# Weight buffers 4,608 bytes apart, and the operands of token-major blocks at one place of a 512-byte line

## The chip, the core and the metric

The kernel runs on one core of one Trainium2 chip. The metric is the time of one execution on the device, in microseconds (us): the median of several runs.

## What is computed

One decoder layer in float32, 256 tokens of 2048 features, with three residual steps: a mixer (chunked mLSTM beside an RWKV-7 scan, each gated and merged), cross-attention into 256 memory tokens, and a convolutional GeGLU network. Nearly all of the arithmetic is projections by large weight matrices:

```python
proj = h @ w_in                                   # 2048 x 10536
merged = sigmoid(g_a) * (ha @ w_branch_a) + sigmoid(g_b) * (hb @ w_branch_b)
y = merged @ w_out                                # 2048 x 2048
q, kv = h @ wq, mem_n @ wkv                       # cross-attention, then o @ wo
u = h @ w_up                                      # 2048 x 16384
uc = conv_b + sum(conv_w[j] * shift_right(u, 2 - j) for j in range(3))
gate, up = split_cols(uc, (8192, 8192))
out = (gelu(gate) * up) @ w_down                  # 8192 x 2048
```

## The kernel before

**Blocks.** The projections are a list of blocks, filled by `block(...)` and worked off in order by `run()` (line 365). Each block has its sources: pieces of a weight matrix of 128 partitions by 1024 float32 values, 512 KB each (the eight of the first block are 768 wide). There are 648 sources. `run()` takes them one after another; a source is called a **weight block** below, and i is its number.

**Staging.** `Feed` streams them. `dma` (line 323) loads weight block i into a raw tile (3 buffers, SP's queue); `hi` (line 339) copies it on ACT into a tile `wh`, rounded to the matmul's format; `lo` (line 348) subtracts on DVE, `wl = raw - wh`, the rest that the rounding lost. Activations come as such a pair too (`hh`/`hl` in the mixer, `mgh`/`mgl` for the merged branches, `mh`/`ml` for the memory tokens, `fh`/`fl` in the network's first matrix, and `as`, which holds both halves, in its second). A product is three matmuls: high by high, low by high, high by low.

**Two kinds of block.** In a feature-major block ("fm") the weights are the stationary operand, 128 by 128, and the activations the moving one, 256 columns: a weight block is 2 x 4 x 3 = 24 matmuls, and each has its own weight load. In a token-major block ("tm", `tm_products`, line 357) it is the other way: the activations are stationary and 512 columns of weights move; a weight block is 12 matmuls. The tm blocks are four blocks of `w_in` (32 weight blocks, i from 72 on, with `hh`/`hl`), the values of the cross-attention (8, with `mh`/`ml`) and the network's second matrix `w_fd` (the last 128, with `as`). The network's first matrix, `w_fu`, is 256 weight blocks of the fm kind, i from 264 to 519.

**Where the tiles lie.** `staged` (line 331) makes the tiles for `wh` and `wl`. Each has four buffers of 1056 float32 values, 4,224 bytes, and the weights begin o values behind the buffer's start: o is 16 (64 bytes) or 24 (96 bytes).

```python
up, down = i - len(self.src) + 384, i - len(self.src) + 128
o = 16 if down >= 0 or i % (16 if up >= 0 else 4) else 24
w = wp.tile([P, 1024 + 32], F32R, tag=name, bufs=4, name=name)
```

So o is 24 for every fourth weight block before `w_fu`, for every sixteenth in `w_fu`, and never in `w_fd`. **Place** below means the first byte's address within a partition, modulo 512. Since 4,224 is 8 x 512 + 128, the four buffers lie at four places 128 bytes apart: in the built program the buffers of `wh` begin at 384, 0, 128 and 256, those of `wl` at the same four, and successive weight blocks use them in the order 384, 256, 128, 0. With o added, the weights of four successive blocks stand at 480, 320, 192 and 64 where the first of the four has o = 24, and at 448, 320, 192 and 64 where it has o = 16. All pieces of a weight block that a matmul reads lie a multiple of 512 bytes from its start, so they have its place.

The activations stand still. `hh`, `hl`, `mh`, `ml`, `fh` and `fl` begin at 384, and every piece that is read has that place; so have the pairs that enter the branches and the last attention matrix (`ha`, `hb`, `oT`); `mgh`, `mgl` and the queries' input `qh`, `ql` begin at 128; `as` (line 1519, two buffers of 4,096 bytes, made by `C`, a helper that gives one buffer for each tag) at 448.

**Order.** PE takes the blocks in program order. Work that is not a block (scan, gates, attention, evacuation of PSUM) is cut into pieces and put between the weight blocks by `side` (`Spread`), by a planned cost of DVE and ACT work. Addresses are no part of that plan. A weight block's first matmul waits for `wh`, its third for `wl`.

Of the kernel before, what the change touches and what calls it, by code (L numbers as in the profile page):

```python
# [10 lines left out]
F32R = mybir.dt.float32r  # L11
# [4 lines left out]
P = 128  # L16
D = 2048
S = 256
# [127 lines left out]
def _layer(ctx, tc, nc, d, dbg):  # L146
# [5 lines left out]
    wp = ctx.enter_context(tc.tile_pool(name="wp", bufs=4))  # L152
    mp = ctx.enter_context(tc.tile_pool(name="mp", bufs=1))
# [14 lines left out]
    def C(name, tag, shape=None, dt=F32):  # L168
        return mp.tile(shape or [P, S], dt, tag=tag, bufs=1, name=name)
# [25 lines left out]
    up = C("up", "bg0", [P, 1024])  # L195
# [35 lines left out]
    def split(hi, lo, src):  # L231
        act.copy(hi, src)
        dve.tensor_sub(lo, src, hi)
# [8 lines left out]
    class Stat:  # L242


        def __init__(self, name, tag="ysb1", sq="au"):
            self.name, self.tag, self.sq = name, tag, sq
            self.rc = cp.tile([P, 2], F32, name=name + "_c")
            self.n = 0
            self.done = False
# [60 lines left out]
    blocks = []  # L310
# [7 lines left out]
    class Feed:  # L318
        def __init__(self):
            self.src = [s for b in blocks for s in b["srcs"]]  # L320
            self.raw, self.st, self.nd, self.ns, self.nl = {}, {}, 0, 0, 0

        def dma(self, upto):
# [6 lines left out]

        def staged(self, name, r, i):

            k, c = r.shape[1:]
            up, down = i - len(self.src) + 384, i - len(self.src) + 128
            o = 16 if down >= 0 or i % (16 if up >= 0 else 4) else 24
            w = wp.tile([P, 1024 + 32], F32R, tag=name, bufs=4, name=name)
            return w[:, o:o + k * c].rearrange("p (k c) -> p k c", k=k)

        def hi(self, upto):
# [1119 lines left out]
    def actile(k):  # L1459
        while len(M["ac"]) <= (k // 16 if k < 32 else 2 + (k - 32) // 8):  # L1460
            n = len(M["ac"])
            M["ac"].append(big("ac") if n < 2 else U("ac"))
        return M["ac"][k // 16][:, k % 16] if k < 32 else M["ac"][2 + (k - 32) // 8][:, (k - 32) % 8]
# [41 lines left out]
    def fu_xs(b):  # L1505
        def xs(k):
            if b == 31 and k == 12:
                asplit(0)
                asplit(2)
            return M["res"].tile(k)  # L1510
        return xs
# [7 lines left out]
    def asplit(k):  # L1519

        if k not in M["as"]:
            n = k // 2
            a = C("as", f"au{n % 2}", [P, 2, 2, S], F32R)
            a, b_ = a[:, 0], a[:, 1]
            for j in range(2):
                split(a[:, j], b_[:, j], actile((k + j) % 64))
                M["as"][k + j] = (a[:, j], b_[:, j])
        return M["as"][k]

    def ax(n):  # L1530
        def xs(k):
            kk = n * 64 + k
            if kk == 58:
                side.need(fu["task"])
            if kk == 24:
                load_gain()
            if k % 2 == 0:
                asplit(kk)
                if kk + 2 < 128 and (k < 62 or n == 0):
                    asplit(kk + 2)  # L1540
            return M["as"].pop(kk)
        return xs
# [176 lines left out]
```

## Time and profile before

| what | value |
|---|---|
| median of 3 runs | 1950.27 us (1949.23 to 1950.96) |
| the profiled execution | 1950.57 us |
| its span, first to last instruction | 1948.7 us |
| mean granted TensorE clock | 0.995 |
| PE busy, matmuls | 1913.3 us, 15,084 of them |
| DVE busy; ACT busy | 1326.8 us; 1000.9 us |

The span is 1.9 us below the execution's own time, and that execution 0.3 us above the median. Matmuls are pipelined: the duration in a row of a matmul reaches from its start to its modelled end, over the start of the next. What one costs is read from the distance between starts.

### The profile page before, as it was taken

Reading aid. Unit: us, or ns where it says so; the run is one execution under the profiler, and the core shown is the slowest. Engines: PE = TensorE matmul, PEld = TensorE weight load, DVE = VectorE, ACT = ScalarE, POOL = GpSimd, SP = SyncE. Lnnn points to the kernel's source line nnn. Section 1 sums busy time; section 2 is a strip of 40 time slices with the busy share of each in tenths; the row PEclk is TensorE's granted clock in tenths of the full one; section 3 lists DMA queues with packets and bytes.
Section 4 is the critical chain, followed back from the end, with each engine's and each line's share of the span. In section 5 each row is a group of like instructions: output and inputs, shape, how many; then the busy total and the mean of one; then the engine's idle time right before and its main releaser. Section 6 shows DMA issues by size and latency. Waiting matters only on the chain.

```text
span 1948.7 us, 36532 instructions
## 1 busy us (share of the span) xinstructions
PE 1913.3 (98%) x15084; PEld 1804.0 (93%) x15084; DVE 1326.8 (68%) x1789; ACT 1000.9 (51%) x1434; POOL 137.5 (7%) x127
## 2 busy tenths in 40 slices
PE   8999999999999999899999999999999999999998
PEld 7999987999999999788999999999999998888886
DVE  7879886566666666867767666766677675556555
ACT  4776434554444565455655444544454454445453
POOL 4213100010100000304000000000000000000000
PEclk9999999999999999999999999999999999999999
DMA  6545554344455675435555555555555555655554
GB/s 207 171 162 168 182 166 152 109 152 141 157 174 184 209 266 175 162 125 173 183 185 185 198 193 194 188 196 196 191 194 189 200 187 203 204 190 188 189 190 151
DMA packets 97607, 352.20 MB, mean 181 GB/s; under 512 B 10881, under 2 KB 11137, under 8 KB 97057
## 3 DMA queue, kind: packets, MB, share of 16 engines
q1 hardware_dynamic: 96496, 348.07, 53.7%
q8 instruction: 118, 1.93, 0.4%
q10 hardware_dynamic: 720, 1.15, 0.2%
q0 software_dynamic: 224, 0.66, 0.1%
q14 instruction: 49, 0.39, 0.1%
HBM read 347.73 MB, written 2.10 MB: 180 GB/s over the span
## 4 chain that ended last, share of the span: by engine, by line
PE 92%; DVE 4%; issue 2%; ACT 1%; DMA 1%; POOL 1%; SPq 0%; DVEq 0%; ACTq 0%; POOLq 0%
PE fm L181 63%; PE tm L181 23%; DVE wl L353 1%; PE Y L181 1%; DVE fl L66 1%; DVE hl L66 1%; PE gram L181 0%; PE lv L181 0%; ACT wh L344 0%; DVE z L66 0%; POOL xr L1221 0%; POOL stx L264 0%; DMA raw<-in_w_sm_dram 0%; DMA raw<-in_w_in_dram 0%; PE num L181 0%
## 5 line engine op out<-in xcount | busy, mean ns | idle before, releaser
L353 DVE TENSOR_TENSOR wl<-raw,wh 128x1024 fp32r<-128x1024 f32 (+1 forms) x648 | 810.6, 1253 | 452.8 <-ACT wh L344 445.3
L344 ACT CAST wh<-raw 128x1024 fp32r<-128x1024 f32 (+1 forms) x648 | 674.7, 1044 | 567.6 <-PE fm L181 385.7
L181 PE MATMUL fm<-fl,wh 128*128 128x256 f32 x2048 | 568.7, 278 | 1.3 <-DVE fl L66 1.3
L181 PE MATMUL fm<-fh,wh 128*128 128x256 f32 x2048 | 569.0, 278 | 0.8 <-ACT fh L66 0.8
L181 PE MATMUL fm<-fh,wl 128*128 128x256 f32 x2048 | 568.1, 277 | 1.1 <-DVE wl L353 1.1
L181 PEld LDWEIGHTS fm<-fl,wh 128*128 128x128 f32 x2048 | 385.3, 188 | 2.1 <-DVE fl L66 1.9
L181 PEld LDWEIGHTS fm<-fh,wl 128*128 128x128 f32 x2048 | 385.5, 188 | 1.2 <-DVE wl L353 1.2
L181 PEld LDWEIGHTS fm<-fh,wh 128*128 128x128 f32 x2048 | 385.5, 188 | 1.0 <-ACT fh L66 1.0
L181 PE MATMUL tm<-wh,as 128*128 128x512 f32 x1024 | 318.7, 392 | 0.0
L181 PE MATMUL fm<-hh,wl 128*128 128x256 f32 x1072 | 302.1, 282 | 11.0 <-DVE wl L353 11.0
L181 PE MATMUL fm<-hh,wh 128*128 128x256 f32 x1072 | 306.0, 285 | 0.5 <-ACT wh L344 0.5
L181 PE MATMUL fm<-hl,wh 128*128 128x256 f32 x1072 | 301.1, 281 | 0.0
L181 PEld LDWEIGHTS tm<-wh,as 128*128 128x128 f32 x1024 | 192.2, 188 | 43.5
L181 PEld LDWEIGHTS fm<-hh,wl 128*128 128x128 f32 x1072 | 203.4, 190 | 13.4 <-DVE wl L353 13.4
L181 PEld LDWEIGHTS fm<-hh,wh 128*128 128x128 f32 x1072 | 203.6, 190 | 3.4 <-ACT wh L344 0.7
L181 PEld LDWEIGHTS fm<-hl,wh 128*128 128x128 f32 x1072 | 203.4, 190 | 0.1
L181 PE MATMUL tm<-wl,as 128*128 128x512 f32 x512 | 201.1, 393 | 0.0
L181 PEld LDWEIGHTS tm<-wl,as 128*128 128x128 f32 x512 | 96.1, 188 | 21.7
L66 ACT CAST as<-ac 128x256 fp32r<-128x256 f32 x128 | 45.6, 404 | 118.0 <-PE tm L181 118.0
L66 DVE TENSOR_TENSOR as<-ac,as 128x256 fp32r<-128x256 f32 x128 | 48.6, 422 | 66.6 <-ACT as L66 66.5
L225 POOL TENSOR_TENSOR rco<-var,mhalf 128x1 f32<-128x1 f32 x2 | 1.1, 551 | 1019.6 <-DVE var L66 1019.6
L181 PE MATMUL fm<-mgh,wh 128*128 128x256 f32 x256 | 71.5, 279 | 0.0
(363 smaller groups left out, 2324.6 us busy)
## 6 DMA issues: line engine op xcount, KB each, us to landing
raw<-in_w_fu_dram SPq DMA_DIRECT2D x256, 512.0 KB, 4.3
raw<-in_w_in_dram SPq DMA_DIRECT2D x160, 512.0 KB, 3.6
raw<-in_w_fd_dram SPq DMA_DIRECT2D x128, 512.0 KB, 4.2
raw<-in_w_br_dram SPq DMA_DIRECT2D x32, 512.0 KB, 3.7
raw<-in_w_mo_dram SPq DMA_DIRECT2D x32, 512.0 KB, 4.2
raw<-in_w_xk_dram SPq DMA_DIRECT2D x8, 512.0 KB, 4.3
raw<-in_w_xq_dram SPq DMA_DIRECT2D x8, 512.0 KB, 3.7
raw<-in_w_xv_dram SPq DMA_DIRECT2D x8, 512.0 KB, 4.0
```

The source lines that it names most:

```text
L66: return f(out, *a, **k)
L181: pe.matmul(out, lhsT, rhs, start=start, stop=stop, skip_group_check=True)
L225: pool.tensor_tensor(out, v, mhalf[:, 0:out.shape[1]], op=ALU.pow)
L344: nc.scalar.copy(wh, r)
L353: nc.vector.tensor_sub(wl, r, self.st[self.nl][0])
```

## The change

It changes places in memory alone. The weight tiles become 1,152 values long, 4,608 bytes, which is 9 x 512: all eight buffers (four of `wh`, four of `wl`) begin at place 384. `staged` sets o by the kind of the block that uses the weights: 0 in tm blocks; in fm blocks 16 or 24 by the old rule. `as` is taken from a buffer longer by 128 values, 112 values (448 bytes) behind its start.

```diff
 class Feed:
     def __init__(self):
         self.src = [s for b in blocks for s in b["srcs"]]
+        self.kind = [b["kind"] for b in blocks for s in b["srcs"]]
...
     def staged(self, name, r, i):
         k, c = r.shape[1:]
-        up, down = i - len(self.src) + 384, i - len(self.src) + 128
-        o = 16 if down >= 0 or i % (16 if up >= 0 else 4) else 24
-        w = wp.tile([P, 1024 + 32], F32R, tag=name, bufs=4, name=name)
+        up = i - len(self.src) + 384
+        o = 0
+        if self.kind[i] == "fm":
+            o = 16 if i % (16 if up >= 0 else 4) else 24
+        w = wp.tile([P, 1024 + 128], F32R, tag=name, bufs=4, name=name)
         return w[:, o:o + k * c].rearrange("p (k c) -> p k c", k=k)
...
     def asplit(k):
         if k not in M["as"]:
             n = k // 2
-            a = C("as", f"au{n % 2}", [P, 2, 2, S], F32R)
+            a = mp.tile([P, 1024 + 128], F32R, tag=f"au{n % 2}", bufs=1, name="as")[:, 112:112 + 1024]
+            a = a.rearrange("p (i j s) -> p i j s", i=2, j=2)
             a, b_ = a[:, 0], a[:, 1]
```

Places before and after, in the built programs:

| blocks | weights before | weights after | activations before | after |
|---|---|---|---|---|
| fm, before `w_fu` | 480, 320, 192, 64 in turn | 480, 448, 448, 448 in turn | 384 or 128 | the same |
| fm, `w_fu` | 448, 320, 192, 64 in turn; 480 for 448 every 16th | 448; 480 every 16th | 384 | 384 |
| tm, `w_in` and values | 480, 320, 192, 64 in turn | 384 | 384 | 384 |
| tm, `w_fd` | 448, 320, 192, 64 in turn | 384 | 448 | 384 |

The instructions, their order on every engine, and what each waits for are the same in both programs. All other tiles move by multiples of 512 bytes and keep their places. The tiles of a partition end at byte 221,348 before and at 225,444 after.

## The prediction

> **What bounds the kernel now.** The page first: which engine is busy, and through which the chain that ended last runs.
>
> ```profile
> span 1948.7 us, 36532 instructions
> ...
> PE 1913.3 (98%) x15084; PEld 1804.0 (93%) x15084; DVE 1326.8 (68%) x1789; ACT 1000.9 (51%) x1434; POOL 137.5 (7%) x127
> ...
> PEclk9999999999999999999999999999999999999999
> ...
> PE 92%; DVE 4%; issue 2%; ACT 1%; DMA 1%; POOL 1%; SPq 0%; DVEq 0%; ACTq 0%; POOLq 0%
> PE fm L181 63%; PE tm L181 23%; DVE wl L353 1%; PE Y L181 1%; DVE fl L66 1%; DVE hl L66 1%; PE gram L181 0%; PE lv L181 0%; ACT wh L344 0%; DVE z L66 0%; POOL xr L1221 0%; POOL stx L264 0%; DMA raw<-in_w_sm_dram 0%; DMA raw<-in_w_in_dram 0%; PE num L181 0%
> ```
>
> PE is the chain: 92% of it, 63% in fm and 23% in tm matmuls, at a granted clock near full all along. The count of matmuls can't change here, so what is left is the distance from the start of one to the start of the next. The busy times by stretches come next (the columns are the stretch, its length, PE, PEld, DVE, ACT, POOL with their counts, clock, DMA): all of the mixer's tm blocks but the first few, its later blocks, 200 weight blocks of `w_fu`, and `w_fd`.
>
> ```profile
> core 0: us, PE busy (x) PEld busy (x) DVE busy (x) ACT busy (x) POOL busy (x), PEclk, DMA share, GB/s
> ...
> 266.70:348.76 82.06, 82.06 (x561) 65.25 (x559) 55.27 (x95) 41.09 (x55) 0.00 (x0) 1.00 0.52 166
> 348.76:669.22 320.46, 318.47 (x3218) 311.23 (x3217) 200.87 (x282) 151.86 (x230) 14.99 (x12) 1.00 0.49 159
> ...
> 1039.85:1586.54 546.69, 546.69 (x4803) 546.69 (x4801) 376.59 (x505) 275.13 (x354) 0.00 (x0) 1.00 0.58 193
> 1586.54:1938.86 352.32, 352.32 (x1533) 287.28 (x1531) 209.88 (x271) 175.76 (x269) 0.55 (x1) 1.00 0.55 187
> ```
>
> In the two stretches of the network PE never stops, and DVE and ACT work 70% of them or less. The third view is the timeline of PE. In it I looked for the first matmul of each weight block: 24 matmuls lie between two of these rows. The first row here is weight block 320, which has o = 24; the blocks stand at 480, 320, 192, 64, 448.
>
> ```profile
> 1039.85 0.28 PE L181 MATMUL fm<-fh,wh 128*128 128x256 f32 x1
> ...
> 1042.67 0.28 PE L181 MATMUL fm<-fh,wh 128*128 128x256 f32 x1
> ...
> 1045.50 0.28 PE L181 MATMUL fm<-fh,wh 128*128 128x256 f32 x1
> ...
> 1048.22 0.28 PE L181 MATMUL fm<-fh,wh 128*128 128x256 f32 x1
> ...
> 1050.94 0.28 PE L181 MATMUL fm<-fh,wh 128*128 128x256 f32 x1
> ```
>
> The same 24 matmuls take 2.82 us at 480, 2.83 at 320, then 2.72 at 192 and 2.72 at 64. No engine is waited for in these stretches; addresses alone differ. The tm blocks of `w_fd` show it too (weight blocks 520 to 522, at 448, 320, 192, with `as` at 448; the second row is the fourth matmul of block 520, the last row the first of block 645):
>
> ```profile
> 1586.54 0.39 PE L181 MATMUL tm<-wh,as 128*128 128x512 f32 x1
> ...
> 1587.23 0.39 PE L181 MATMUL tm<-wh,as 128*128 128x512 f32 x1
> ...
> 1589.27 0.40 PE L181 MATMUL tm<-wh,as 128*128 128x512 f32 x1
> ...
> 1592.07 0.39 PE L181 MATMUL tm<-wh,as 128*128 128x512 f32 x1
> ...
> 1931.93 0.40 PE L181 MATMUL tm<-wh,as 128*128 128x512 f32 x1
> ```
>
> Where weights and `as` share a place the block takes 2.73 us, and its last nine matmuls 2.04 (1587.23 to 1589.27), 0.227 each; 128 bytes apart it takes 2.80. So I read: PE's distance between starts depends on where its two operands stand to each other, by 2 to 4%, and PE is the bound. The rest is what each place costs.
>
> **tm blocks of the network.** After the change every weight block of `w_fd` has the difference of block 520: none. Its first three matmuls took 0.69 us, more than 3 x 0.227, which I put down to the slow block ahead; between equal blocks that goes. A block then takes 12 x 0.227 = 2.72. Now the 125 blocks from 1586.54 to 1931.93 take 345.39; at 2.72 they take 340.0. Term: -5.4 (the last three blocks, done bank by bank, are left as they are). Its ends: -6 if they gain as well, -4 if the first matmuls of a block stay slow.
>
> One rule of the Trainium skill speaks against this term and all the others: "TensorE: Matmul & The Clock Gate" (Step-by-step: what each phase is for) gives PE two independent read ports, so that a weight load takes nothing from the running matmul, and "SBUF — State Buffer" (SBUF: two separate sides) says that PE never waits on anyone there. By that rule places don't matter and the change gives 0. The trace disagrees: 2.73 against 2.80 us for equal work. I keep the rows.
>
> **tm blocks of the mixer and the values.** Four blocks of the mixer, 480, 320, 192 and 64 against 384:
>
> ```profile
> 266.70 0.39 PE L181 MATMUL tm<-wh,hh 128*128 128x512 f32 x1
> ...
> 277.85 0.39 PE L181 MATMUL tm<-wh,hh 128*128 128x512 f32 x1
> ```
>
> They take 11.15 us, 2.79 each; after the change 384 against 384, again no difference, so 2.72. That is 0.07 x 40 blocks = 2.8 at most. Later blocks of the stage are broken up by other matmuls (561 in 82.06 us), after which a block starts anew, so I take -2.5, with -1.5 and -2.8 as ends.
>
> **fm blocks.** Here the change isn't aimed at a better place: 448 against 384 is a difference that exists, and 480 stays. What goes is the step of 128 bytes from one weight block to the next. The trace has a row that makes this the open question. Weight blocks 274, 275 and 276, at 192, 64 and 448; block 272 stood at 480, 273 at 320:
>
> ```profile
> 905.00 0.28 PE L181 MATMUL fm<-fh,wh 128*128 128x256 f32 x1
> ...
> 907.83 0.28 PE L181 MATMUL fm<-fh,wh 128*128 128x256 f32 x1
> ...
> 910.65 0.28 PE L181 MATMUL fm<-fh,wh 128*128 128x256 f32 x1
> ```
>
> Block 274 takes 2.83 at 192, where block 322 took 2.72. So a place doesn't fix the pace: there are two paces at one place, each holds through a whole weight block, and where nothing else comes between, it changes at a block's start, where the place steps. The block at 480 sets the slow pace, and a later step, at the second block behind it (1045.50) or the fourth (910.65), ends it. After the change there are two steps only, into 480 and out of it to 448, 32 bytes each. Either the step out sets the fast pace, and it holds until the next 480 or a wait of PE; or it leaves the slow one, and nothing then ends it.
>
> Bounds for the 200 blocks of `w_fu`: all fast they take 544.0 (-2.7 from 546.69), all slow 200 x 2.825 = 565 (+18.3). With the step out fast, 12 or 13 blocks at 480 stay slow by 0.10, and the blocks at 320 no longer follow: -1.4. In the blocks before `w_fu` every fourth is at 480 and its successor slow too:
>
> ```profile
> 669.22 0.28 PE L181 MATMUL fm<-mgh,wh 128*128 128x256 f32 x1
> ...
> 674.87 0.28 PE L181 MATMUL fm<-mgh,wh 128*128 128x256 f32 x1
> ...
> 680.31 0.28 PE L181 MATMUL fm<-mgh,wh 128*128 128x256 f32 x1
> ```
>
> Two blocks in 5.65, two in 5.44: half are slow where nothing disturbs. With one in four slow, 216 fm blocks gain 54 x 0.10 = 5.4 at most. Most of them lie among other matmuls (in 348.76 to 669.22 there are 3218 for 96 weight blocks, which have 2304), and a slow pace after such a break would now last until the next 480. I take -2, ends -5.4 and +3. Which of the two cases holds, no row shows: 480 to 448 doesn't occur before. I lean to the fast case, since 192 and 448, which have the difference of the new place or differ from it by 256, are where the slow pace ended: at 1045.50 and at 910.65.
>
> **What hides the rest.** DVE and ACT write and read the moved tiles. Their time per weight block in `w_fu`:
>
> ```profile
> L353 DVE TENSOR_TENSOR wl<-raw,wh 128x1024 fp32r<-128x1024 f32 x200 | 244.8, 1224 | 166.5 <-ACT wh L344 166.5
> L344 ACT CAST wh<-raw 128x1024 fp32r<-128x1024 f32 x200 | 209.5, 1048 | 249.1 <-PE fm L181 248.5
> ```
>
> 1.22 and 1.05 us against 2.72 of PE: if the new places cost or gave them a tenth, PE would not see it; uncovered, a tenth of DVE's would be 0.12 x 648 = 79 us, but DVE works 376.59 of 546.69 us there. The order, the waits and the transfers stay, so nothing new is waited for.
>
> **Sum.** -5.4 - 2.5 - 1.4 - 2 = -11.3 against the profiled 1950.57, which is 0.3 above the median: 1950.3 - 11.3 = 1939. Ends of this case: -6 - 2.8 - 2.7 - 5.4 = -17, or 1933; and -4 - 1.5 with fm blocks 3 worse, or 1948.
>
> **Rivals.**
>
> 1. *The slow pace stays* (slower). Place: the first weight block behind each 480. Price: 0.10 for each fm block that is fast now: +18.3 in the 200 blocks, some +3 in the 56 blocks of `w_fu` before them, and of the 216 before those at most half, 108 x 0.10 = 11; with waits that now and then set the fast pace I take 6. With the tm gain of 7.9: +19, or 1969 (1962 to 1974). It decides the sign once some 80 fast blocks are lost. For it: block 274's row, and that the block at 320, straight behind 480, is slow (1042.67). Against: 320 differs from 384 by another amount than 448 does.
>
> 2. *Mixed*: the step out sets now one pace, now the other, by how the matmuls before it fell. Half the loss, +14, against 7.9: 1950 to 1958, centre 1953.
>
> 3. *Places are not the cause*; the pace alternates with the buffers for another reason, and nothing changes: 1950. Against it stands that 2.73 and 2.80 follow the place through all of `w_fd`, and 480 through `w_fu`. This is what the skill's rule of independent ports would give.
>
> **How the numbers follow.** Forecast 0.55, rival 1 0.33, rival 2 0.08, rival 3 0.04. About 0.2%, 3.9 us, is what a measurement of this kernel can tell from no change, so faster is under 1946.4, slower above 1954.2. Faster: 0.55 less 0.02 for the forecast's weak end, and 0.01 of rival 2: 0.54. Same: 0.02, rival 3's 0.04 and 0.04 of rival 2: 0.10. Slower: 0.33 and 0.03: 0.36. Leaving out no more than 0.2 takes in rival 1 up to its centre and a little: 1934 to 1970. The forecast's own range is 1934 to 1946.
>
> **What would show it.** Right: rows of `w_fd` 2.72 apart from block to block, without alternation, and `w_fd` to the same last block in 340; tm blocks of the mixer near 2.72; in `w_fu` 2.82 at every sixteenth block and 2.72 at the one behind it. If that one takes 2.83 and the fourteen after it too, rival 1 holds, and the stretch of 200 blocks is 565 long. If `w_fd` still alternates, my reading of the tm rows was wrong.

## The result, and the profile after

The changed kernel takes 1939.91 us (median of 4 runs, 1937.59 to 1940.45), the kernel before 1950.59 beside it (4 runs, 1949.23 to 1950.96): a ratio of 0.9939, interval 0.9928 to 0.9951. The forecast was 1939. The profiled execution took 1939.58 us, with a span of 1937.6.

The page of the changed kernel: engines, granted clock and chain.

```profile
span 1937.6 us, 36532 instructions
...
PE 1900.6 (98%) x15084; PEld 1798.7 (93%) x15084; DVE 1326.1 (68%) x1789; ACT 1001.6 (52%) x1434; POOL 137.1 (7%) x127
...
PEclk9999999999999999999999999999999999999999
...
PE 87%; DVE 5%; ACT 2%; issue 2%; DMA 2%; POOL 1%; DVEq 0%; SPq 0%; ACTq 0%; POOLq 0%
PE fm L181 59%; PE tm L181 23%; DVE wl L357 2%; ACT wh L348 1%; DMA raw<-in_w_in_dram 1%; DVE fl L66 1%; PE Y L181 1%; DMA raw<-in_w_fu_dram 0%; PE gram L181 0%; PE lv L181 0%; DVE z L66 0%; POOL xr L1225 0%; POOL stx L264 0%; DMA x<-in_x_dram 0%; DVE BK L66 0%
```

The counts are the same, the clock too, and PE is still what ends last. PE's busy time fell by 12.7 us; that of DVE and ACT moved by 0.7 each. Stretches of the kernel before that the prediction didn't show, cut at block starts: the whole of the mixer's tm blocks, and the first 56 weight blocks of `w_fu`.

```profile
238.73:348.76 110.03, 110.03 (x742) 88.05 (x740) 76.03 (x131) 49.51 (x63) 1.29 (x1) 1.00 0.49 157
...
872.85:1039.85 167.00, 162.63 (x1384) 161.52 (x1385) 122.27 (x157) 90.36 (x125) 21.61 (x14) 0.99 0.53 177
```

The same view of the changed kernel: the mixer's tm blocks, weight blocks 104 to 199, the first 56 of `w_fu`, its other 200, and the 125 of `w_fd`.

```profile
238.46:346.88 108.42, 108.42 (x742) 88.01 (x740) 75.98 (x131) 49.56 (x63) 1.30 (x1) 1.00 0.52 160
346.88:667.27 320.39, 318.55 (x3219) 311.35 (x3218) 200.81 (x282) 151.87 (x230) 14.99 (x12) 0.99 0.51 159
...
870.08:1034.62 164.54, 161.30 (x1385) 160.39 (x1385) 122.05 (x157) 90.29 (x125) 21.56 (x14) 0.98 0.54 180
1034.62:1580.87 546.25, 546.25 (x4803) 546.25 (x4801) 376.63 (x505) 275.28 (x354) 0.00 (x0) 1.00 0.59 193
1580.87:1920.89 340.02, 340.02 (x1502) 281.55 (x1501) 207.01 (x265) 174.71 (x263) 0.00 (x0) 1.00 0.57 194
```

Cut at the same block starts in both traces, the difference lies here (us):

| weight blocks | before | after | difference | term |
|---|---|---|---|---|
| `w_fd`, 520 to 644 (tm) | 345.39 | 340.02 | -5.4 | -5.4 |
| mixer 72 to 103 and values 248 to 255 (tm) | 110.03 + 33.16 | 108.42 + 32.87 | -1.9 | -2.5 |
| `w_fu`, last 200 (fm) | 546.69 | 546.25 | -0.4 | -1.4 |
| other fm blocks ahead of `w_fu` | | | -1.1 | -2 |
| `w_fu`, first 56 (fm) | 167.00 | 164.54 | -2.5 | none |

They add up to -11.3; the spans differ by 11.1. Of the -1.9, the mixer has -1.6 and the values -0.3; the values' share is no larger than their scatter between kernels with the same places (32.3 to 32.9 us with the weights at 384), and so isn't shown by itself.

Part of the last row is not pace: PE's idle time in that stretch (its length less PE's busy time) fell from 4.4 to 3.2 us.

The timeline of PE in `w_fd`: the first matmuls of weight blocks 520 to 524, and of 271.50 and 282.38, four blocks of the mixer apart ("x2" joins two matmuls of one kind).

```profile
271.50 0.39 PE L181 MATMUL tm<-wh,hh 128*128 128x512 f32 x1
...
282.38 0.39 PE L181 MATMUL tm<-wh,hh 128*128 128x512 f32 x1
...
1580.87 0.63 PE L181 MATMUL tm<-wh,as 128*128 128x512 f32 x2
...
1583.61 0.62 PE L181 MATMUL tm<-wh,as 128*128 128x512 f32 x2
...
1586.33 0.62 PE L181 MATMUL tm<-wh,as 128*128 128x512 f32 x2
...
1589.05 0.62 PE L181 MATMUL tm<-wh,as 128*128 128x512 f32 x2
...
1591.77 0.39 PE L181 MATMUL tm<-wh,as 128*128 128x512 f32 x1
```

2.74, then 2.72 from block to block: the alternation of 2.73 and 2.80 is gone. What alternated there shows one thing more. In the kernel before, weight block 522 stood at 192, 256 bytes from `as`; it began at 1592.07, and block 523 here:

```profile
1594.80 0.40 PE L181 MATMUL tm<-wh,as 128*128 128x512 f32 x1
```

Block 522 took 2.73, as block 520 did at the place of `as`. So 256 bytes apart was as fast as none, only the blocks at 320 and 64 (128 and 384 apart) were slow: as far as these four distances show, what counts for these blocks is the place in 256 bytes, not in 512.

Four blocks of the mixer take 10.88 where they took 11.15. In `w_fu`, weight blocks 320 to 323 (320 stands at 480, the others at 448), then 336 (at 480) to 338:

```profile
1034.62 0.28 PE L181 MATMUL fm<-fh,wh 128*128 128x256 f32 x1
...
1037.50 0.28 PE L181 MATMUL fm<-fh,wh 128*128 128x256 f32 x1
...
1040.23 0.28 PE L181 MATMUL fm<-fh,wh 128*128 128x256 f32 x1
...
1042.95 0.28 PE L181 MATMUL fm<-fh,wh 128*128 128x256 f32 x1
...
1078.31 0.28 PE L181 MATMUL fm<-fh,wh 128*128 128x256 f32 x1
...
1081.19 0.28 PE L181 MATMUL fm<-fh,wh 128*128 128x256 f32 x1
...
1083.92 0.28 PE L181 MATMUL fm<-fh,wh 128*128 128x256 f32 x1
```

The block at 480 now takes 2.88 (it was 2.82), the one behind it 2.73, and then 2.72. So the fast pace (2.72 us a block, 113.3 ns a matmul) comes back by itself behind a 480, as forecast; but the 480 became dearer. DVE and ACT, per weight block in the same 200 blocks:

```profile
L357 DVE TENSOR_TENSOR wl<-raw,wh 128x1024 fp32r<-128x1024 f32 x200 | 244.8, 1224 | 166.1 <-ACT wh L348 165.9
L348 ACT CAST wh<-raw 128x1024 fp32r<-128x1024 f32 x200 | 209.7, 1049 | 248.5 <-PE fm L181 248.3
```

1224 and 1049 ns, where they were 1224 and 1048: their time did not change with the places.

### The profile page after: what moved, and what is told of

Same layout as the page of the kernel before. It is cut to its first block, busy times and chain, and to the rows that moved or that the text cites. A ratio compares the mean times of both kernels' runs of the same rounds, so it can differ in the third digit from the quotient of the medians.

```text
span 1937.6 us, 36532 instructions
## 1 busy us (share of the span) xinstructions
PE 1900.6 (98%) x15084; PEld 1798.7 (93%) x15084; DVE 1326.1 (68%) x1789; ACT 1001.6 (52%) x1434; POOL 137.1 (7%) x127
## 4 chain that ended last, share of the span: by engine, by line
PE 87%; DVE 5%; ACT 2%; issue 2%; DMA 2%; POOL 1%; DVEq 0%; SPq 0%; ACTq 0%; POOLq 0%
PE fm L181 59%; PE tm L181 23%; DVE wl L357 2%; ACT wh L348 1%; DMA raw<-in_w_in_dram 1%; DVE fl L66 1%; PE Y L181 1%; DMA raw<-in_w_fu_dram 0%; PE gram L181 0%; PE lv L181 0%; DVE z L66 0%; POOL xr L1225 0%; POOL stx L264 0%; DMA x<-in_x_dram 0%; DVE BK L66 0%
## 5 line engine op out<-in xcount | busy, mean ns | idle before, releaser
L181 PE MATMUL fm<-hh,wl 128*128 128x256 f32 x1072 | 301.7, 281 | 11.9 <-DVE wl L357 11.9
```

Source lines behind the costliest of these rows:

```text
L181: pe.matmul(out, lhsT, rhs, start=start, stop=stop, skip_group_check=True)
```

## The experiments

**Theory**: the distance between the places of PE's two operands sets how far apart matmuls start, and of the change only the tm part matters much. **Rivals**: the step of 128 bytes from block to block does it; a block at 480 is needed to get out of a slow pace; the absolute place of one operand does it. All diffs are against the changed kernel; in `staged`, o = 0, 16, 24 and 32 give places 384, 448, 480 and 0. The first four kernels ran together, beside the kernel before at 1951.5 us.

**tm_only.** The fm weights back at their old places.

```diff
-                o = 16 if i % (16 if up >= 0 else 4) else 24
+                o = (16, 112, 80, 48)[i % 4]
+                if i % (16 if up >= 0 else 4) == 0:
+                    o = 24
```

> fm weights at the old places (480 or 448, 320, 192, 64 in turn), tm blocks as in the change. If the two parts act apart, this keeps the tm gain alone: w_fd from block 520 to block 645 in 340 us (345.4 before), the mixer's tm blocks 1.6 us less, the values' 0.3, and the fm stretches as before (200 blocks of w_fu in 546.7). 1950.6 - 7.3 = 1943.3 us. If the spacing of the buffers mattered by itself, the fm stretches would move as well.

Measured: 1942.86 us (1942.14 to 1943.52), ratio 0.9956 (0.9943 to 0.9968). `w_fu`'s last 200 blocks and `w_fd`'s 125:

```profile
1038.05:1584.73 546.68, 546.68 (x4802) 546.68 (x4801) 376.57 (x505) 275.20 (x354) 0.00 (x0) 1.00 0.62 193
1584.73:1924.76 340.03, 340.03 (x1503) 281.54 (x1501) 206.89 (x265) 174.80 (x263) 0.00 (x0) 1.00 0.61 194
```

`w_fu` is as before the change (546.69), `w_fd` as after it: the longer buffers by themselves give the fm blocks nothing. The tm part alone carries 8.6 us.

**fm_only.** The reverse: tm weights and `as` at their old places.

```diff
-            o = 0
+            down = i - len(self.src) + 128
+            o = (16 if down >= 0 else 24, 112, 80, 48)[i % 4]
...
-            a = mp.tile([P, 1024 + 128], F32R, tag=f"au{n % 2}", bufs=1, name="as")[:, 112:112 + 1024]
+            a = mp.tile([P, 1024 + 128], F32R, tag=f"au{n % 2}", bufs=1, name="as")[:, 0:0 + 1024]
```

> fm blocks as in the change, tm blocks at the old places with as at 448. If the two parts act apart: w_fd alternates 2.73 and 2.79 us per block again (345.4), the fm stretches are those of the change, 3.9 us less than before in all: 1946.7 us. If the gain in fm came from elsewhere, for instance from tm blocks that end earlier, it is missing: 1950.

Measured: 1948.24 us (11 runs, 1944.09 to 1949.88), ratio 0.9978 (0.9969 to 0.9987). The mixer's tm blocks, `w_fu` and `w_fd`:

```profile
238.03:348.06 110.03, 110.03 (x742) 88.00 (x740) 76.08 (x131) 49.55 (x63) 1.30 (x1) 1.00 0.52 158
1034.91:1581.16 546.25, 546.25 (x4803) 546.25 (x4801) 376.65 (x505) 275.33 (x354) 0.00 (x0) 1.00 0.62 193
1581.16:1926.55 345.39, 345.39 (x1503) 281.56 (x1502) 207.07 (x265) 174.14 (x263) 0.00 (x0) 1.00 0.60 191
```

110.03 and 345.39 are the values before the change, to the digit, and 546.25 that of after. The fm part is worth 3.3 us here, and the two parts together (8.6 + 3.3) make 11.9, where the whole change measured 10.7; the intervals hold both.

**no_96.** No block at 480: every fm block at 448, tm at 384.

```diff
-            o = 0
-            if self.kind[i] == "fm":
-                o = 16 if i % (16 if up >= 0 else 4) else 24
+            o = 16 if self.kind[i] == "fm" else 0
```

> The change without the blocks at 480: every fm block at 448. Theory: the blocks at 480 cost 2.88 us instead of 2.72 and serve only to end a slow pace; behind the last wait in w_fu the pace is fast already, so the 200 blocks take 544.0 instead of 546.2. Before w_fu some 54 of them go, 0.16 each, up to 8.6 us, but a slow pace that a break sets lasts until the next break: 1932 to 1940, 1936 taken. Rival: without them nothing ends the slow pace, and it holds through most fm blocks: w_fu 200 blocks 565, 1960 or more.

Measured: 1933.91 us (1930.47 to 1934.79), ratio 0.9903 (0.9890 to 0.9917), faster than both kernels. Weight blocks 104 to 199 and `w_fu`'s last 200:

```profile
345.60:662.93 317.33, 315.20 (x3218) 307.97 (x3217) 200.65 (x282) 151.84 (x230) 14.99 (x12) 0.99 0.52 160
1032.03:1576.03 544.00, 544.00 (x4802) 544.00 (x4801) 376.64 (x505) 273.97 (x354) 0.00 (x0) 1.00 0.63 194
```

544.00 is 4800 matmuls at 113.33 ns: no slow one is left, and here the 480s only cost. The first 56 weight blocks of `w_fu` are longer than in the changed kernel (164.54), and most of that is waiting: PE is idle for 5.3 us of them, where it was 3.2.

```profile
864.13:1032.03 167.90, 162.56 (x1384) 161.35 (x1385) 122.15 (x157) 90.38 (x125) 21.57 (x14) 0.98 0.55 175
```

Ahead of `w_fu` there still are stretches at the slow pace (2.83 us a block, 117.7 ns a matmul). Weight blocks 40 to 42, the first of four `ssk` matmuls (work that is not a block) between blocks 44 and 45, and blocks 46 to 48, all at 448:

```profile
137.06 0.28 PE L181 MATMUL fm<-hh,wh 128*128 128x256 f32 x1
...
139.88 0.28 PE L181 MATMUL fm<-hh,wh 128*128 128x256 f32 x1
...
142.71 0.28 PE L181 MATMUL fm<-hh,wh 128*128 128x256 f32 x1
...
151.19 0.28 PE L181 MATMUL ssk<-hsh,bones 128*128 128x256 f32 x1
...
154.40 0.28 PE L181 MATMUL fm<-hh,wh 128*128 128x256 f32 x1
...
157.12 0.28 PE L181 MATMUL fm<-hh,wh 128*128 128x256 f32 x1
...
159.84 0.28 PE L181 MATMUL fm<-hh,wh 128*128 128x256 f32 x1
```

2.82 and 2.83, then, behind four `ssk` matmuls, 2.72 and 2.72: two paces at one place, and the pace changes where other matmuls stand in between, without any 480 or step.

**tm_128.** The tm weights 128 bytes from their activations, all at one place.

```diff
-            o = 0
+            o = 32
```

> tm weights at 512 (o = 32), 128 bytes behind the place of the activations, all blocks alike; fm as in the change. If the difference of places sets the pace, each block of w_fd takes 2.80 us, 125 blocks 350 us against 340.0, and the tm blocks of the mixer 2.80: 1940 + 10 + 2.5 = 1952 us. Rival: the step from one block's place to the next costs, not the difference: then 340.0 again and 1940 us.

Measured: 1950.94 us (1947.76 to 1952.69), ratio 0.9995 (0.9986 to 1.0004). The mixer's tm blocks and `w_fd`:

```profile
238.36:348.43 110.07, 110.07 (x742) 88.22 (x740) 76.09 (x131) 49.50 (x63) 1.29 (x1) 1.00 0.52 158
1585.10:1933.67 348.57, 348.57 (x1502) 282.62 (x1501) 207.16 (x265) 174.10 (x263) 0.00 (x0) 1.00 0.60 189
```

The whole gain of the tm part is gone, with no step from block to block, and `w_fd` takes 3.2 us more than before the change (345.39), where every second block, at 448 or 192, had been fast; that eats up what the fm part gives. So it is the distance, not the stepping, that the tm blocks pay for.

The next four ran together, beside the kernel before at 1951.68 us.

**tm_both.** Weights as in tm_128, and `as` moved by 128 bytes too: in `w_fd` both stand at place 0, in the mixer they are 128 apart.

```diff
-            o = 0
+            o = 32
...
-            a = mp.tile([P, 1024 + 128], F32R, tag=f"au{n % 2}", bufs=1, name="as")[:, 112:112 + 1024]
+            a = mp.tile([P, 1024 + 128], F32R, tag=f"au{n % 2}", bufs=1, name="as")[:, 16:16 + 1024]
```

> In the blocks of w_fd both the streamed weights and the stationary activations are moved by 128 bytes, to place 0; in the token-major blocks of the mixer and the values only the weights are, so those are 128 apart there (110.1 us for the mixer, as before the change). If the distance between the two sets the pace, w_fd takes 340.0 us up to its last three blocks, and the whole is 1942 us (1939 to 1945). If the place of the weights or of the activations by itself does, it takes 345 to 349 us and the whole is 1947 to 1952 us.

Measured: 1940.15 us (1939.55 to 1940.93), ratio 0.9939 (0.9924 to 0.9954).

```profile
237.93:348.00 110.07, 110.07 (x743) 88.21 (x741) 76.01 (x131) 49.54 (x63) 1.29 (x1) 1.00 0.52 158
...
1581.83:1921.83 340.00, 340.00 (x1503) 281.53 (x1501) 206.85 (x265) 174.19 (x263) 0.00 (x0) 1.00 0.61 194
```

The mixer is slow, `w_fd` is at 340.0 again, with the same weights as in tm_128: the distance between the operands decides in the tm blocks, the absolute place doesn't.

**steps_no_96.** Feature-major weights through 448, 320, 192 and 64 in turn, none at 480.

```diff
-                o = 16 if i % (16 if up >= 0 else 4) else 24
+                o = (16, 112, 80, 48)[i % 4]
```

> Feature-major weights go through 448, 320, 192 and 64 in turn with no block at 480, token-major ones at 384. If the steps to another place are what starts the slow pace of 117.7 ns and only a block at 480 ended it, the last 200 blocks of w_fu are slow nearly throughout: 565 us instead of 546.7, and the whole is about 1960 us (1950 to 1975). If a block at 480 only costs (0.1 to 0.15 us each) and the slow stretches end by themselves, the whole is 1937 us (1933 to 1942), between the kernel with all weights at 448 and the one with the old places.

Measured: 1935.48 us (1934.84 to 1936.15), ratio 0.9915 (0.9900 to 0.9930). `w_fu`'s last 200 blocks, and the timeline of weight blocks 320 to 324, at 448, 320, 192, 64 and 448:

```profile
1032.13:1576.13 544.00, 544.00 (x4802) 544.00 (x4801) 376.56 (x505) 273.88 (x354) 0.00 (x0) 1.00 0.61 194
```

```profile
1032.13 0.28 PE L181 MATMUL fm<-fh,wh 128*128 128x256 f32 x1
...
1034.85 0.28 PE L181 MATMUL fm<-fh,wh 128*128 128x256 f32 x1
...
1037.57 0.28 PE L181 MATMUL fm<-fh,wh 128*128 128x256 f32 x1
...
1040.29 0.28 PE L181 MATMUL fm<-fh,wh 128*128 128x256 f32 x1
...
1043.01 0.28 PE L181 MATMUL fm<-fh,wh 128*128 128x256 f32 x1
```

2.72 at each of the four places. The steps cost nothing, and 320 is as fast as 192: in the kernel before it was slow where it followed 480. The four places differ from 384 by 64 or by 64 and a multiple of 128.

**fm_0 and fm_96.** All fm blocks at 384, at no distance from the activations; all at 480, 96 from them. The edit of fm_0, with 24 for the 0 in fm_96:

```diff
-                o = 16 if i % (16 if up >= 0 else 4) else 24
+                o = 0
```

> Every block at place 384: the stationary weights of the feature-major blocks lie at the place of the activations (384), as in token-major blocks, and nothing lies at 480. If the relative place alone sets the pace in both kinds of block, equal places are the best ones and the feature-major blocks stay at 113.3 ns a matmul: the last 200 blocks of w_fu take 200 x 24 x 113.3 ns = 544 us, as with all of them at 448, and the whole is 1934 us (1930 to 1940). If feature-major blocks want their stationary weights 64 bytes from the activations, they go at 117.7 ns: the 200 blocks take 565 us and, with the 216 feature-major blocks ahead and the first 56 of w_fu mostly at that pace too, the whole is 1965 to 1980 us.

> All feature-major weights at 480 (96 bytes from the activations), token-major ones at 384. The blocks at 480 in the changed kernel had 117 to 122 ns from one matmul to the next. If the place itself has that price, the last 200 blocks of w_fu take 200 x 24 x 120 ns = 576 us (565 at 117.7), and the whole is 1970 to 1995 us. If only the entry into 480 from another place was dear, the blocks run at 113.3 ns once they follow each other: 544 us there, and 1934 to 1940 us in the whole.

Measured: fm_0 1989.78 us (1989.22 to 1990.01), ratio 1.0193 (1.0177 to 1.0208); fm_96 1974.38 (1972.79 to 1976.87), ratio 1.0117 (1.0100 to 1.0134). `w_fu`'s last 200 blocks in fm_0:

```profile
1055.02:1631.02 576.00, 576.00 (x4803) 576.00 (x4801) 378.17 (x505) 275.97 (x354) 0.00 (x0) 1.00 0.57 183
```

And in fm_96:

```profile
1045.31:1614.91 569.60, 569.60 (x4802) 569.60 (x4801) 377.50 (x505) 276.15 (x354) 0.00 (x0) 1.00 0.58 185
```

Equal places, the best for tm blocks, are bad for fm blocks: 576.00 / 4800 = 120.0 ns a matmul, worse than either value I had for it, and the whole is beyond both ranges. My idea that one rule holds for both kinds fell here. 480 costs 118.7 ns as long as blocks stay there, not only on entry.

The last three ran together, beside the kernel before at 1949.87 us.

**fm_32, fm_48, fm_80.** The same edit with o = 8, 12 and 20: fm weights 32, 48 and 80 bytes from the activations.

> All feature-major weights at 416, 32 bytes from the activations at 384; token-major ones at 384. So far, with all feature-major weights at one place, 0 bytes apart ran at 120.0 ns a matmul (last 200 blocks of w_fu 576.0 us), 64 apart at 113.3 ns (544.0 us) and 96 apart at 118.7 ns (569.6 us). If the price depends on how far the distance is from 64 on either side, 32 apart is like 96: 118.7 ns, 569.6 us for the 200 blocks and 1974 us (1970 to 1980) in the whole. If only equal places collide, it is 113.3 ns: 544 us and 1934 us.

> All feature-major weights at 432, 48 bytes from the activations. If the price falls off evenly to both sides of 64 apart (0 at 64, 5.3 ns at 96), 48 apart costs 2.7 ns a matmul: 116.0 ns, 557 us for the last 200 blocks of w_fu, 1954 us in the whole (1945 to 1965). If there is a window of fast distances about 64, they stay at 113.3 ns, 544.0 us and 1934 us; and if the slow stretches ahead of w_fu at 64 apart hang on the exact distance, these get fewer or more (1930 to 1950).

> All feature-major weights at 464, 80 bytes from the activations. If the price is even on both sides of 64, the same as at 48 apart: 116.0 ns, 557 us and 1954 us (1945 to 1965) if it rises evenly, 544.0 us and 1934 us if there is a window. If it is not even, the two kernels differ in these 200 blocks, by up to 20 us.

Measured: fm_32 1975.26 us (1974.79 to 1975.92), ratio 1.0128 (1.0113 to 1.0143); fm_48 1989.15 (1972.47 to 2004.44), ratio 1.0170 (1.0098 to 1.0242); fm_80 1976.74 (1976.21 to 1977.36), ratio 1.0136 (1.0119 to 1.0153). The 200 blocks in fm_32:

```profile
1048.85:1616.85 568.00, 568.00 (x4802) 568.00 (x4801) 377.19 (x505) 276.46 (x354) 0.00 (x0) 1.00 0.58 186
```

In fm_48:

```profile
1050.74:1642.73 591.99, 591.99 (x4802) 591.99 (x4801) 381.13 (x505) 276.02 (x354) 0.00 (x0) 1.00 0.55 178
```

In fm_80:

```profile
1047.97:1617.57 569.60, 569.60 (x4802) 569.60 (x4801) 377.44 (x505) 276.17 (x354) 0.00 (x0) 1.00 0.58 185
```

Per matmul: 118.3 ns at 32 bytes, 123.3 at 48, 113.3 at 64, 118.7 at 80 and at 96. There is neither a window about 64 nor, in these profiles, an even rise, so those expectations for 48 and 80 missed; 48 and 80 differ by 22.4 us, as the third case for 80 had it, a little beyond its 20. Of the distances tried, 64 alone is fast. fm_48's four runs were 1972.47, 1976.96, 2001.33 and 2004.44, too far apart for one price; the ratio leaves out the last. The profile is of the one at 2001.33, so 123.3 belongs to its slower runs; what a matmul took in the faster two is in no trace.

## Why the prediction was right, step by step

**What bounds it: right.** The large gains and losses above are PE's distance between starts, in stretches where PE never stops. Ahead of `w_fu` and in its first 56 blocks PE also waits, and there the waits blur what the distances give.

**tm blocks of `w_fd`: right in mechanism and size.** -5.4 forecast, -5.4 measured; the slow first matmuls did go with the slow block ahead. The term was taken from the measured 345.39, so it did not need to know that only every second block was slow. That the distance is the cause is shown by tm_128 (gain gone) and tm_both (gain back at another place).

**tm blocks of the mixer and values: right, mis-sized.** -1.9 for -2.5, inside the term's ends, and only the mixer's -1.6 of it is clear: the stretch of 32 blocks took 110.03 to 110.07 us in the four kernels with the tm weights off 384 and 108.4 to 108.5 in all others. An undisturbed block does gain the forecast 0.07 (10.88 against 11.15 for four); the blocks broken up by other matmuls gain less than I allowed.

**The 200 blocks of `w_fu`: the case was right, its size wrong.** -0.4 for -1.4. The step out of 480 gave the fast pace, as taken. The term kept the old price of a block at 480, 0.10; it is 2.88 - 2.72 = 0.16 now. 13 blocks x 0.06 = 0.8 of the missing 1.0. Why it is dearer when entered from 448 than from 64 wasn't tried. What gained is the block behind each 480 (2.73 for 2.83), not the steps that went: steps cost nothing in steps_no_96.

**The other fm blocks.** -1.1 for -2 ahead of `w_fu`, and -2.5 in the first 56 blocks of it, for which the sum had no term. That last number isn't all the change's: tm_128, fm_only and tm_both, with the same fm places, take 166.3, 165.4 and 166.3 us there (164.5 in the changed kernel), and tm_only, with the old ones, 166.6. So a part of the close hit in the whole is luck. fm_only's 3.3 us is the better measure of what all fm blocks gain together, the first 56 of `w_fu` included (-3.4 forecast, without a term for these).

The pace itself gained more than -1.1 ahead of `w_fu`. Taking only distances of at most 125 ns from one fm matmul to the next, what they have over 113.3 ns adds up to 15.8 us there before and 12.1 after, -3.7 for the forecast's -2 (15.6 in tm_only; 12.0, 11.7 and 11.5 in fm_only, tm_128 and tm_both). Everything else in these stretches, waits and other matmuls, took some 2.7 us more, and no run shows why. So the term was too small for what it described, and what it left out hid that.

**The reason I gave for the fast case was wrong.** I read 480 as what sets the slow pace and a later step as what ends it, and leaned to the fast case because slow stretches had ended at 192 and 448. steps_no_96 shows 448, 320, 192 and 64 equally fast. Nor does 320 differ from 384 by another amount than 448 does, as rival 1 had it: both are 64 away, to the two sides. The 480s were read rightly as slow, but not as something that could be left out; without them the kernel takes 1934 us.

**Rivals.** The slow pace doesn't stay: 546.25, not 565, which leaves no room for rival 2's mixture in `w_fu` either (13 blocks x 0.16 make 2.1 of the 2.25 over 544.0). Rival 1 needed 480 to be followed by a pace that nothing ends; in `w_fu` it ends within a block. Ahead of `w_fu`, stretches at the slow pace do last several blocks (no_96's rows), which is what the rival described, but in those rows they end where other matmuls stand between the blocks. That places are not the cause fell with tm_128 and fm_0; the Trainium skill's rule in "SBUF — State Buffer" (SBUF: two separate sides), by which PE waits for no one there, does not cover 544.00 against 576.00 us for the same 4800 matmuls.

What stays open: what in PE makes the distance matter, and what picks the pace behind a break at distance 64. No run here shows either.

## What to carry to other kernels

Where PE is the bound, read the distance from start to start for each address of its two operands: equal work at two paces, with every other engine idle part of the time, points at where the tiles lie. Here streamed weights wanted the place of their stationary activations, or one 256 bytes off, and stationary weights a place 64 bytes from that of the moving ones; find the distance by trying each kind of block by itself. An offset that is there in every nth block may be a leftover: leave it out once before building on it.

## What the runs showed that I had not expected

- Of the distances tried, the best differs by the kind of block: none for 512 moving columns (340.0 us for 125 blocks, 348.6 at 128 bytes; a block 256 bytes apart was as fast as one at none before the change), 64 bytes for 256 moving columns with 24 weight loads a block (544.0 us for 200 blocks; 576.0 at none).
- 16 bytes decide: 113.3 ns at 64 bytes, 123.3 (in the profiled run) at 48, 118.7 at 80.
- At one place and one order the pace can be either of two, and hold for blocks: 2.72 and 2.83 us in no_96. The whole of fm_48, 1972 or 2004 us, may be another case; no trace of its faster runs shows it.
- The kernel without 480s takes 1933.91 us against the changed kernel's 1939.91 (0.9903 and 0.9939 of the kernel before, each beside its own runs of it), and the 6 us come from a line that the change kept.
